# An encoder trunk on one core: ScalarE's weight casts ordered behind sigmoids, VectorE's combinations ordered behind low parts, sums of squares taken ahead, and last stores in finer pieces

## Chip, cores and metric

The kernel runs on one core of one Trainium2 chip. The metric is the device time of one execution in microseconds. Shorter is better. Engines are named as in the profile: PE is TensorE, DVE is VectorE, ACT is ScalarE, POOL is GpSimd, and SP is the engine that issues most DMAs.

## What is computed

One layer of a bidirectional hybrid encoder on x of shape (1, 1024, 1024), everything in float32. Cut to what matters here:

```python
h = rmsnorm(x)
proj = h @ w_in                       # 8192 columns: gated unit, q, v, z_f, z_b, gates
a = glu(glu_in)                       # values * sigmoid(gates), 512 columns
a = dwconv31(a); a = silu(layernorm(a)); a = a @ pw_w
o = bi_hgrn2(q, v, z_f, z_b)          # gated linear recurrence in both directions
b = (headnorm(o) * silu(og)) @ o_w
x = x + (sigmoid(g_a) * a + sigmoid(g_b) * b) @ w_out
x = x + (silu(dwconv3(h2 @ w_gate)) * (h2 @ w_up)) @ w_down     # h2 = rmsnorm(x)
return rmsnorm(x)                     # the last norm, the last stage of the kernel
```

## The kernel before

Activations are kept transposed, with features on the 128 partitions and positions along the row, in two halves of 512 positions. A product of float32 precision is made of three passes of TensorE: every weight and every activation is split into a high part (a cast on ScalarE) and a low part (the source minus the high part, on VectorE). The helper `split` (line 123, its instructions at L124) issues both, and `mm3` (L148, L149, L150) the three matmuls: high by high, high by low, low by high. So a weight's low part is first needed by the third matmul of a job.

The program goes through stages: first norm, gated unit, the other projections ("pairs") with the depthwise convolution on VectorE beside them, layer norm, scan of the heads, output projections, feed-forward network up and down, last norm. TensorE's instructions run exactly in the order in which the program emits them. The other engines' orders are made by a planner at compile time from its own cost model. Once made, each engine's order is fixed, and each engine waits in order. `pin` keeps single instructions in program order, and `tc.issue_after(ins)` makes every instruction of its block that is on the engine of `ins` follow `ins` in that engine's order. It adds no wait on another engine.

**Gated unit (`glu_jobs`, line 916).** There are four groups of 128 columns, 0 to 3. For each group and half there is a gate job and a value job (`glu_tiles`, line 863), each of 24 matmuls into one bank tagged "mm", of which there are three. At the end of a gate job `evac_b` (line 848) applies the sigmoid on ScalarE (L851) from the bank into a page of the tag "tm", of which there are four. At the end of a value job `evac_a` (line 855) multiplies bank and page on VectorE (L857). The first half of all groups and the second half of group 3 run first, while the second norm is still going on; the second halves of groups 0, 1 and 2 come last, as six jobs: gate 0, value 0, gate 1, value 1, gate 2, value 2. In the texts below "gate job 1" means gates of group 1, second half.

`run_jobs` (line 194) prepares a job's weights (`std_job`, line 250: a 512 KB load into one of two "wr" pages, then a split into two of four "wp" pages) just after the job before it has been started in program order. So when the weights of gate job 1 are prepared, the last sigmoid that has been emitted is that of gate job 0. Two "wp" pages belong to a job, so a cast can't run before the job two places ahead has used its pages for the last time.

**Combinations (`h_combos`, line 937).** The pairs use a product scheme with seven products in place of eight. Their operands are sums and differences of quarters of h. For each of four blocks k, three quarters are loaded from DRAM into pages "su" (four of them) and `combos` (line 461) makes three combinations on VectorE (L466), each of which is then split. All four are emitted ahead of the last 17 steps of the gated unit:

```python
p1 = tc.alloc_tile_pool(name="p1", bufs=1, reuse_waits="tile")
h_combos()
s_glu.fill(GLU_LATE)          # GLU_LATE = 17
pair0 = in_pair(0)
w_pair0 = pair0[0]()          # weights of the first pair
s_glu.drain()
```

**Convolution (`conv_steps`, line 1028).** 31 taps of 1024 positions for each of four groups on VectorE (L1036, L1039), emitted between steps of the pairs. A pair's results are evicted by VectorE too (L800), and some by ScalarE. The convolved rows go out to DRAM (`d_cv`) and come back for the layer norm (first sums at L1051 and L1053).

**Last norm (`turn_out`, `finish`, `scale_out`, lines 1904 to 1960).** The last matmuls make blocks of 128 features for groups of 128 positions ("chunks"); the very last part has the second half's chunks 2 and 3, for i = 0 to 7 in turn. Each block is transposed by TensorE (L1912), ScalarE squares it and adds up (L1914), and VectorE applies the gain (L1929). After block 7 a reduction over the eight sums (L1920), a scaling (L1923) and a power on GpSimd (L1924) give the reciprocal root. Then `scale_out` multiplies each chunk, 640 columns on VectorE (L1957) and 384 on ScalarE (L1955), and stores it (L1959, 512 KB). `finish(*PARTS[-1], late=0)` does so for the last two chunks, and with their stores the kernel ends.

Of the kernel before, what the change touches and what calls it, by code (L numbers as in the profile page):

```python
# [10 lines left out]
F32 = mybir.dt.float32  # L11
# [3 lines left out]
AF = mybir.ActivationFunctionType  # L15
ALU = mybir.AluOpType
AX = mybir.AxisListType

P = 128
# [10 lines left out]
GLU_LATE = 17  # L30
ALIGN = 128
H = 512
EPS = 1e-6
# [14 lines left out]
def tile_hybrid_encoder(  # L48
# [22 lines left out]
    nc = tc.nc  # L71
    PSUM = bass.MemoryType.PSUM
    V, A, G, T = nc.vector, nc.scalar, nc.gpsimd, nc.tensor

    S, D = x.shape[1], x.shape[2]
    ND = D // P
    CW = conv_dw_w.shape[2]
# [8 lines left out]
    cp = ctx.enter_context(tc.tile_pool(name="const", bufs=1))  # L86
# [7 lines left out]
    def nm(s):  # L94
        uid[0] += 1
        return f"{s}_{uid[0]}"
# [3 lines left out]
    def bank(tag):  # L100
        return ps.tile([P, H], F32, tag=tag, name=nm(tag), bufs=BANKS[tag])

    def page(pool, tag, bufs, dt=F32):
        return pool.tile([P, H], dt, tag=tag, name=nm(tag), bufs=bufs)

    def tmp():
        return page(mp, "tm", 4)
# [13 lines left out]
    pin = tc.keep_in_program_order  # L121

    def split(hi, lo, src, eng, late=False):
        parts = A.copy(hi, src), eng.tensor_tensor(lo, src, hi.bitcast(F32), op=ALU.subtract)  # L124
        if late:
            for i in parts:
                pin(i)
        return hi, lo

    def w_cols(w, r0, nk, c0, cols=P):  # L130
        return w[0, r0 : r0 + nk * P, c0 : c0 + cols].rearrange("(k p) e -> p k e", p=P)

    def raw_w(src, nk):
        t = mp.tile([P, nk, P], F32, tag="wr", name=nm("wr"), bufs=2)
        nc.sync.dma_start(t, src)
        return t

    def w_page(nk, pool=None):
        if pool is None:
            return mp.tile([P, nk, P], F32R, tag="wp", name=nm("wp"), bufs=4)  # L140
        return pool.tile([P, nk, P], F32R, tag="wq", name=nm("wq"), bufs=3)

    def mm3(acc, w, act, k, first, last, again=False):


        whi, wlo = w
        ahi, alo = act
        T.matmul(acc, whi[:, k, :], ahi, start=first, stop=False, skip_group_check=again)  # L148
        T.matmul(acc, whi[:, k, :], alo, start=False, stop=False, skip_group_check=again)  # L149
        T.matmul(acc, wlo[:, k, :], ahi, start=False, stop=last, skip_group_check=again)  # L150
# [99 lines left out]
    def std_job(src, nk, acts, evac, halves=(0, 1), step=2):  # L250


        def prep():
            raw = raw_w(src, nk)
            return split(w_page(nk), w_page(nk), raw, V)

        def run(w, halves=halves):
            for half in halves:
                acc = bank("mm")
                for k in range(nk):  # L260
                    mm3(acc, w, acts(k, half), k, k == 0, k == nk - 1)
                    if k % step == step - 1 or k == nk - 1:
                        yield
                evac(half, acc)

        return prep, run
# [194 lines left out]
    def combos(ops, k, b11, b12, b22, alloc):  # L461

        def sub(o, a, b):
            V.tensor_tensor(o, a, b, op=ALU.subtract)  # L466

        def parts(i, src):
            ops[i].append(split(alloc(), alloc(), src, V))

        t3 = page(mp, "tm", 4)
        sub(t3, b12, b22)
        parts(7, t3)
        sub(b22, t3, b11)
        parts(6, b22)
        sub(b12, b11, b12)
        parts(5, b12)
# [104 lines left out]
    def in_cols(c0):  # L582
        return w_cols(w_in, 0, ND, c0)
# [3 lines left out]
    ht = {i: [] for i in range(1, 8)}  # L587
# [256 lines left out]

    gate = {}
    early = []

    def evac_b(j):
        def evac(hf, acc):
            gate[j, hf] = tmp()  # L850
            A.activation(gate[j, hf], acc, AF.Sigmoid)  # L851

        return evac

    def evac_a(j):
        def evac(hf, acc):
            V.tensor_tensor(  # L857
                gl[j][:, PAD + hf * H : PAD + (hf + 1) * H], acc, gate.pop((j, hf)), op=ALU.mult
            )

        return evac

    def glu_tiles(j, halves):
        yield std_job(in_cols(CW + j * P), ND, h_std, evac_b(j), halves)
        yield std_job(in_cols(j * P), ND, h_std, evac_a(j), halves)

    glu_raw, glu_w = [], []

# [47 lines left out]
    def glu_jobs():  # L916
        def loaded(job, key, pages):
            def prep():
                return split(pages(), pages(), early[key], V)

            return prep, job[1]

        def early_page():
            return p0.tile([P, ND, P], F32R, tag="xn", name=nm("wp"), bufs=4)

        yield glu_first()
        job0, job1 = glu_tiles(1, (0,))
        yield loaded(job0, 0, early_page)
        yield loaded(job1, 1, lambda: w_page(ND))
        job0, job1 = glu_tiles(2, (0,))  # L930
        yield loaded(job0, 2, lambda: w_page(ND))
        yield job1
        yield from glu_tiles(3, (0, 1))
        for j in (0, 1, 2):
            yield from glu_tiles(j, (1,))

    def h_combos():
        def hy():
            return page(p1, "hy", 24, F32R)

        for k in range(NK2):
            b11, b12, b22 = (page(p1, "su", 4) for _ in range(3))
            for t, (kk, half) in ((b11, (k, 0)), (b12, (k, 1)), (b22, (k + NK2, 1))):
                nc.sync.dma_start(t, d_h[kk][half])
            combos(ht, k, b11, b12, b22, hy)

    s_glu = Stream(run_jobs(glu_jobs(), prime=1, first=GLU_LEAD))
    s_glu.fill()
    ahead = p0.tile([P, ND, P], F32, name="ahead")
# [13 lines left out]
    s_glu.fill(GLU_MORE)  # L963
    p0.release()
    p1 = tc.alloc_tile_pool(name="p1", bufs=1, reuse_waits="tile")
    h_combos()
    s_glu.fill(GLU_LATE)
    pair0 = in_pair(0)
    w_pair0 = pair0[0]()
    s_glu.drain()  # L970
# [85 lines left out]
    for half in range(2):  # L1056
# [18 lines left out]
        rs = next(rstd)  # L1075
# [387 lines left out]
    for h in range(NH):  # L1463
# [4 lines left out]
        for half in range(2):  # L1468
            i = 2 * h + half
# [238 lines left out]
    for k in range(NK2):  # L1708
        s_out.fill(16 if k else 17) if k < NK2 - 1 else s_out.drain()
        b11, b12, b21, b22 = x2[k][0], x2[k][1], x2[k + NK2][0], x2[k + NK2][1]  # L1710
# [193 lines left out]
    def turn_out(i, half, chunks):  # L1904

        t, n = xr[i][half], len(chunks)
        if i == 0 and chunks[0] == 0:
            out_y.append(fy.tile([P, 4, D], F32, tag="y", name=nm("y"), bufs=2))
        ss, y = out_ss[half], out_y[half]
        b = bank(next(y_tags))[:, : n * P]  # L1910
        for m, c in enumerate(chunks):
            T.transpose(b[:, m * P : (m + 1) * P], t[:, c * P : (c + 1) * P], ident)  # L1912
        for m, c in enumerate(chunks):
            A.activation(  # L1914
                out_junk[c % 2], b[:, m * P : (m + 1) * P], AF.Square, accum_out=ss[:, i, c : c + 1]
            )
        those = slice(chunks[0], chunks[-1] + 1)
        if i == ND - 1:
            rs = cp.tile([P, 4], F32, name=nm("frs"), tag="frs", bufs=2)[:, :n]
            V.tensor_reduce(  # L1920
                rs, ss[:, :, those].rearrange("p i c -> p c i"), axis=AX.X, op=ALU.add
            )
            V.tensor_scalar(rs, rs, 1.0 / D, EPS, op0=ALU.mult, op1=ALU.add)  # L1923
            G.tensor_tensor(rs, rs, mhalf.to_broadcast([P, n]), op=ALU.pow)  # L1924
            for m, c in enumerate(chunks):
                out_r[half, c] = rs[:, m : m + 1]

        def gain():
            return V.tensor_tensor(  # L1929
                y[:, those, i * P : (i + 1) * P],  # L1930
                b.rearrange("p (c e) -> p c e", e=P),
                view(fnw, i * P, [[0, n], [1, P]]),
                op=ALU.mult,
            )

        if i == ND - 3 and half and chunks[-1] == 3:
            gains.append(gain)
        elif i == ND - 1:
            pin(gain())
        else:  # L1940
            gain()
# [7 lines left out]

    def scale_out(half, c):  # L1950
        y, r = out_y[half], out_r[half, c]
        for o, cols in ((0, 640), (640, D - 640)):
            sl = slice(o, o + cols)
            if o:
                pin(A.activation(y[:, c, sl], y[:, c, sl], AF.Copy, scale=r))  # L1955
            else:
                pin(V.tensor_scalar(y[:, c, sl], y[:, c, sl], r, None, op0=ALU.mult))  # L1957
        n = half * 4 + c
        nc.sync.dma_start(out[0, n * P : (n + 1) * P, :], y[:, c, :])  # L1959

    out_y, out_r = [], {}
    per_std, per_seven = 2 * ((FIRST + 1) // 2), 7 * ((NS + 1) // 2)
    jobs = std_down(0, FIRST, first_evac)
    first_seven = seven_down(0)[0]
# [53 lines left out]
    n = starts[-1] - per_seven - 12  # L2018
# [50 lines left out]
```

## Time and profile before

| | us |
|---|---|
| median of 3 runs | 1721.52 (1721.14 to 1722.52) |
| the profiled execution's own time | 1721.94 |
| its span in the trace | 1720.0 |
| TensorE busy in the span | 1699.1 |
| VectorE busy | 1256.6 |
| ScalarE busy | 825.0 |
| GpSimd busy | 240.7 |

The span is what the trace covers; the execution's own time has 1.94 us more around it. A row of a timeline gives start and duration in us, engine, line, operation and operands by tile name; in brackets stands how long the engine sat idle before it and what ended that. In the list of waits a row says who waited for whom, for how long in all, how often, and the longest. A row of a table by stretches has the stretch, its length, the busy time of TensorE, weight loads, VectorE, ScalarE and GpSimd with the number of instructions, then TensorE's granted clock, the share of the DMA engines and GB/s. "SPq" is a DMA issue on SP's queue.

### The profile page before, as it was taken

What the parts mean: (1) busy time and instruction counts of PE and PEld (TensorE: products, weight loads), DVE (VectorE), ACT (ScalarE), POOL (GpSimd) and SP (SyncE); (2) the same over time, 40 slices, a digit from 0 to 9 for tenths busy, and PEclk for the clock granted to TensorE, in tenths of its full rate; (3) what the DMA queues carried; (4) which work ended last, traced back from release to release, by engine and by line L of the source; (5) the groups of instructions that cost most, each with busy time, mean ns of one, the idle gap of its engine ahead of it and who ended that gap; (6) DMA issues with size and microseconds to landing.
All of it is one profiled execution on the core that took longest, in us unless ns stands there. A gap on an engine that the chain in (4) does not pass through costs nothing.

```text
span 1720.0 us, 30762 instructions
## 1 busy us (share of the span) xinstructions
PE 1699.1 (99%) x11902; PEld 1416.2 (82%) x11902; DVE 1256.6 (73%) x1937; ACT 825.0 (48%) x1544; POOL 240.7 (14%) x281
## 2 busy tenths in 40 slices
PE   8999999999999999999999999999999999999998
PEld 6878888788788888888888888888888888888787
DVE  4599999745779888888656466667777776657865
ACT  6443443233577777776442245444434433542334
POOL 1212222200001111111100002122222222000110
PEclk9999999999999999999999999999999999999999
DMA  8777888854673444435689466577778776783842
GB/s 281 238 181 177 201 191 189 203 160 148 202 261 91 146 127 133 128 116 200 223 277 279 143 205 199 147 159 153 165 166 174 171 172 154 229 266 102 215 95 99
DMA packets 337096, 308.28 MB, mean 179 GB/s; under 512 B 17582, under 2 KB 249142, under 8 KB 336950
## 3 DMA queue, kind: packets, MB, share of 16 engines
q1 hardware_dynamic: 289590, 267.51, 49.1%
q0 software_dynamic: 47360, 38.81, 15.5%
q8 instruction: 93, 1.52, 0.4%
q14 instruction: 53, 0.43, 0.1%
HBM read 201.40 MB, written 87.03 MB: 168 GB/s over the span
## 4 chain that ended last, share of the span: by engine, by line
PE 61%; DVE 1%; ACT 1%; DMA 0%; issue 0%; POOLq 0%; ACTq 0%; SPq 0%; DVEq 0%
PE mm L148 14%; PE mm L150 14%; PE mm L149 14%; PE sc L148 3%; PE sc L150 3%; PE sc L149 3%; PE ob L1375 2%; PE tr L148 1%; PE tr L150 1%; PE tr L149 1%; PE sc L1197 1%; PE sc L1283 1%; PE mm L1334 1%; PE sc L1334 1%; PE ob L1197 0%
## 5 line engine op out<-in xcount | busy, mean ns | idle before, releaser
L148 PE MATMUL mm<-hx,wp 128*128 128x512 f32 x1068 | 426.9, 400 | 2.3 <-ACT tm L851 1.4
L150 PE MATMUL mm<-hx,wp 128*128 128x512 f32 x1068 | 416.9, 390 | 0.5 <-DVE wp L124 0.5
L149 PE MATMUL mm<-hx,wp 128*128 128x512 f32 x1068 | 416.2, 390 | 0.0
L124 ACT CAST wp<-wr 128x1024 fp32r<-128x1024 f32 (+2 forms) x147 | 147.3, 1003 | 217.8 <-PE mm L149 180.3
L148 PEld LDWEIGHTS mm<-hx,wp 128*128 128x128 f32 x1068 | 200.6, 188 | 45.0 <-DVE ev L800 2.2
L150 PEld LDWEIGHTS mm<-hx,wp 128*128 128x128 f32 x1068 | 200.5, 188 | 44.4 <-DVE wp L124 1.6
L149 PEld LDWEIGHTS mm<-hx,wp 128*128 128x128 f32 x1068 | 200.8, 188 | 39.2 <-issue 0.7
L124 DVE TENSOR_TENSOR wp<-wr,wp 128x1024 fp32r<-128x1024 f32 (+2 forms) x145 | 169.1, 1167 | 39.1 <-ACT wp L124 32.7
L1039 DVE SCALAR_TENSOR_TENSOR acc<-gl,v_b,acc 128x1024 f32<-128x1024 f32 x120 | 148.7, 1272 | 0.4
L440 ACT COPY su<-mm 128x512 f32<-128x512 f32 x82 | 47.7, 582 | 80.1 <-PE mm L150 80.1
L1315 POOL DMA_DIRECT2D S<-D x64 | 36.3, 573 | 284.2 <-ACT S L1313 155.6
L1144 DVE TENSOR_TENSOR qF<-qF,tb 128x512 f32<-128x512 f32 x96 | 65.5, 684 | 13.3 <-ACT A L1178 12.7
L124 ACT CAST wq<-sw 128x1024 fp32r<-128x1024 f32 x41 | 43.2, 1053 | 61.2 <-PE mm L149 32.9
L148 PE MATMUL tr<-hx,wp 128*128 128x512 f32 x180 | 70.5, 392 | 0.0
L150 PE MATMUL tr<-hx,wp 128*128 128x512 f32 x180 | 70.1, 389 | 0.0
L149 PE MATMUL tr<-hx,wp 128*128 128x512 f32 x180 | 70.0, 389 | 0.0
L1144 DVE TENSOR_TENSOR kG<-kG,tb 128x512 f32<-128x512 f32 x96 | 65.5, 685 | 4.7 <-ACT A L1178 2.5
L1652 DVE SCALAR_TENSOR_TENSOR tm<-gp,v_a,tm 128x512 f32<-128x512 f32 x88 | 66.0, 750 | 4.0 <-ACT tm L1650 2.0
L301 POOL DMA_DIRECT2D sw<-in_ffn_w_up_dram x38 | 49.8, 1498 | 116.5 <-DMA sw<-in_ffn_w_up_dram 76.7
L148 PE MATMUL mm<-hy,wp 128*128 128x512 f32 x164 | 64.2, 391 | 0.0
L148 PE MATMUL sc<-hy,wq 128*128 128x512 f32 x164 | 64.2, 391 | 0.0
L150 PE MATMUL sc<-hy,wq 128*128 128x512 f32 x164 | 63.8, 389 | 0.0
(375 smaller groups left out, 3723.3 us busy)
## 6 DMA issues: line engine op xcount, KB each, us to landing
wr<-in_w_in_dram SPq DMA_DIRECT2D x48, 512.0 KB, 5.0
wr<-in_ffn_w_up_dram SPq DMA_DIRECT2D x22, 512.0 KB, 5.1
sw<-in_w_in_dram SPq DMA_DIRECT2D x38, 256.0 KB
d_g<-ft SPq DMA_DIRECT2D x38, 256.0 KB, 2.0
sw<-in_ffn_w_up_dram SPq DMA_DIRECT2D x38, 256.0 KB, 3.5
sw<-in_ffn_w_up_dram POOLq DMA_DIRECT2D x38, 256.0 KB, 6.2
wr<-sw POOLq DMA_DIRECT2D x32, 256.0 KB, 3.3
wr<-wr POOLq DMA_DIRECT2D x32, 256.0 KB, 3.4
```

The costliest lines, as they stand in the source:

```text
L124: parts = A.copy(hi, src), eng.tensor_tensor(lo, src, hi.bitcast(F32), op=ALU.subtract)
L148: T.matmul(acc, whi[:, k, :], ahi, start=first, stop=False, skip_group_check=again)
L149: T.matmul(acc, whi[:, k, :], alo, start=False, stop=False, skip_group_check=again)
L150: T.matmul(acc, wlo[:, k, :], ahi, start=False, stop=last, skip_group_check=again)
L301: G.dma_start(o, a, accum_op=ALU.add)
L440: A.copy(t, acc)
L1039: V.scalar_tensor_tensor(acc, g[:, k : k + S], tap(k), acc, op0=ALU.mult, op1=ALU.add)
L1144: return V.tensor_tensor(o, a, b, op=op)
L1315: G.dma_start(S_t[g : g + 32, :, g : g + 32], D_t[g : g + 32])
L1334: T.matmul(u[:, sl], kTs[d][:, sl], v[:, c, :], start=True, stop=True)
L1375: T.matmul(o[:, sl], l, r, start=(n == 0), stop=(n == len(terms) - 1))
L1652: V.scalar_tensor_tensor(c, g[:, o + k : o + k + H], vec("fdw", k * NF + j), c, op0=ALU.mult, op1=ALU.add,)
```

## The change

Four edits, which add no TensorE work:

1. Each weight preparation of the six last jobs of the gated unit is wrapped in `behind_gate`: the cast must follow, on ScalarE, the sigmoid that was emitted last.
2. For value job 1 and gate job 2 the low part's instruction is kept (`kept_lo`). The combinations of block 2 must follow, on VectorE, the low part of value job 1, and those of block 3 the low part of gate job 2. So that these exist, the gated unit's steps are emitted in between; the later fill is shortened by as many steps.
3. The sums of squares of blocks 0 to 6 are reduced, scaled and given the epsilon when block 6 is done; after block 7 one operation adds the last square to that.
4. In the very last part, chunk 2 is scaled and stored in two pieces, 320 columns on VectorE first, then the rest.

```diff
     gate = {}
     early = []
+    last_gate, last_lo = [], []
...
             gate[j, hf] = tmp()
-            A.activation(gate[j, hf], acc, AF.Sigmoid)
+            last_gate[:] = [A.activation(gate[j, hf], acc, AF.Sigmoid)]
...
+    def behind_gate(job):
+        def prep():
+            with tc.issue_after(last_gate[0].ins):
+                return job[0]()
+
+        return prep, job[1]
+
+    def kept_lo(src, job):
+        def prep():
+            raw, hi, lo = raw_w(src, ND), w_page(ND), w_page(ND)
+            A.copy(hi, raw)
+            last_lo.append(V.tensor_tensor(lo, raw, hi.bitcast(F32), op=ALU.subtract))
+            return hi, lo
+
+        return prep, job[1]
...
         for j in (0, 1, 2):
-            yield from glu_tiles(j, (1,))
+            job0, job1 = glu_tiles(j, (1,))
+            yield behind_gate(kept_lo(in_cols(CW + j * P), job0) if j == 2 else job0)
+            yield behind_gate(kept_lo(in_cols(j * P), job1) if j == 1 else job1)
...
-            combos(ht, k, b11, b12, b22, hy)
+            if k >= 2:
+                while len(last_lo) < k - 1:
+                    s_glu.fill()
+                    fills.append(k)
+                with tc.issue_after(last_lo[k - 2].ins):
+                    combos(ht, k, b11, b12, b22, hy)
+            else:
+                combos(ht, k, b11, b12, b22, hy)
...
+    fills = []
     h_combos()
-    s_glu.fill(GLU_LATE)
+    s_glu.fill(GLU_LATE - len(fills))
...
+        if i == ND - 2:
+            part = cp.tile([P, 4], F32, name=nm("fpt"), tag="fpt", bufs=2)[:, :n]
+            V.tensor_reduce(
+                part, ss[:, : ND - 1, those].rearrange("p i c -> p c i"), axis=AX.X, op=ALU.add
+            )
+            V.tensor_scalar(part, part, 1.0 / D, EPS, op0=ALU.mult, op1=ALU.add)
+            out_part[half, chunks[0]] = part
         if i == ND - 1:
             rs = cp.tile([P, 4], F32, name=nm("frs"), tag="frs", bufs=2)[:, :n]
-            V.tensor_reduce(
-                rs, ss[:, :, those].rearrange("p i c -> p c i"), axis=AX.X, op=ALU.add
+            V.scalar_tensor_tensor(
+                rs,
+                ss[:, i, those],
+                1.0 / D,
+                out_part.pop((half, chunks[0])),
+                op0=ALU.mult,
+                op1=ALU.add,
             )
-            V.tensor_scalar(rs, rs, 1.0 / D, EPS, op0=ALU.mult, op1=ALU.add)
...
-        for o, cols in ((0, 640), (640, D - 640)):
+        n = half * 4 + c
+        rows = out[0, n * P : (n + 1) * P, :]
+        early = 320 if half and c == 2 else 0
+        if early:
+            pin(V.tensor_scalar(y[:, c, :early], y[:, c, :early], r, None, op0=ALU.mult))
+            nc.sync.dma_start(rows[:, :early], y[:, c, :early])
+        for o, cols in ((early, 640 - early), (640, D - 640)):
             sl = slice(o, o + cols)
-            if o:
+            if o == 640:
...
-        n = half * 4 + c
-        nc.sync.dma_start(out[0, n * P : (n + 1) * P, :], y[:, c, :])
+        nc.sync.dma_start(rows[:, early:], y[:, c, early:])
```

More of the change, by code (lines that the diff above doesn't have):

```diff
@@ L1957, in scale_out @@
                 pin(V.tensor_scalar(y[:, c, sl], y[:, c, sl], r, None, op0=ALU.mult))
-        n = half * 4 + c
-        nc.sync.dma_start(out[0, n * P : (n + 1) * P, :], y[:, c, :])
-    out_y, out_r = [], {}
+        nc.sync.dma_start(rows[:, early:], y[:, c, early:])
+    out_y, out_r, out_part = [], {}, {}
     per_std, per_seven = 2 * ((FIRST + 1) // 2), 7 * ((NS + 1) // 2)
```

## Prediction

> **What bounds the kernel now.** I read the totals of the page first, then the list of whom TensorE waited for, then the stretches.
>
> ```profile
> PE 1699.1 (99%) x11902; PEld 1416.2 (82%) x11902; DVE 1256.6 (73%) x1937; ACT 825.0 (48%) x1544; POOL 240.7 (14%) x281
> ```
>
> TensorE is busy 1699.1 of 1720.0 us, and the change touches none of its instructions. So only stalls can go, about 21 us in all. Two stretches (columns: stretch, its length, then busy time of TensorE, weight loads, VectorE, ScalarE, GpSimd) hold most of them, 6.5 at the start and 8.3 at the end:
>
> ```profile
> 0.00:20.00 20.00, 13.51 (x48) 10.32 (x49) 9.13 (x19) 12.79 (x23) 6.50 (x22) 1.00 0.95 305
> ...
> 1680.00:1720.00 40.00, 31.75 (x252) 30.38 (x250) 20.20 (x52) 17.39 (x96) 2.42 (x3) 0.93 0.27 106
> ```
>
> The list of waits, for TensorE alone, names the one stall that the gated unit owns:
>
> ```profile
> PE mm L148 <- ACT tm L851: 1.4, 1, 1.4
> ...
> PE mm L148 <- DVE ev L800: 0.7, 1, 0.7
> ```
>
> The timelines of TensorE and of ScalarE show its place (columns: start, duration, engine, line, what):
>
> ```profile
> 95.77 0.39 PE L149 MATMUL mm<-hx,wp 128*128 128x512 f32 x1
> 96.00 0.39 PE L150 MATMUL mm<-hx,wp 128*128 128x512 f32 x1
> 97.84 0.50 PE L148 MATMUL mm<-hx,wp 128*128 128x512 f32 x1 [1.45 <-ACT tm L851]
> ```
>
> ```profile
> 68.38 1.05 ACT L124 CAST wp<-wr 128x1024 fp32r<-128x1024 f32 x1 [3.30 <-PE mm L149]
> 74.20 0.60 ACT L851 ACTIVATE tm<-mm 128x512 f32<-128x512 f32 x1 [4.76 <-PE ob L519]
> ...
> 85.43 1.05 ACT L124 CAST wp<-wr 128x1024 fp32r<-128x1024 f32 x1
> ...
> 90.80 1.05 ACT L124 CAST wp<-wr 128x1024 fp32r<-128x1024 f32 x1 [3.28 <-PE mm L149]
> ...
> 96.24 1.04 ACT L124 CAST wp<-wr 128x1024 fp32r<-128x1024 f32 x1
> 97.19 1.08 ACT L851 ACTIVATE tm<-mm 128x512 f32<-128x512 f32 x2
> ```
>
> Two sigmoids run together at 97.19. The first belongs to gate job 0 (second half). Its sums were complete when the cast at 85.43 started, because that cast waits for the same job to free its weight page. The sigmoid stands behind three more weight casts in ScalarE's order and holds one of three "mm" banks until 97.7, so value job 1 can't start. Matmuls follow each other here at 0.23 us, so from 96.00 to 97.84 the loss is 1.84 - 0.23 = **1.61 us**.
>
> Next, VectorE:
>
> ```profile
> 120.00:240.00 120.00, 120.00 (x531) 99.35 (x530) 119.72 (x130) 50.67 (x72) 27.82 (x26) 1.00 0.84 190
> ```
>
> The third busy number is VectorE: 119.72 of 120. In the convolution stage it is as full as TensorE, and three rows show the two tied together at its end:
>
> ```profile
> 327.52 2.60 DVE L1039 SCALAR_TENSOR_TENSOR acc<-gl,v_b,acc 128x1024 f32<-128x1024 f32 x2
> ...
> 339.54 0.69 DVE L1053 TENSOR_TENSOR tm<-tm,cx 128x512 f32<-128x512 f32 x1 [6.50 <-DMA cx<-d_cv]
> ...
> 341.15 0.68 DVE L800 TENSOR_TENSOR ev<-su,mm 128x512 f32<-128x512 f32 x1
> ```
>
> ```profile
> 341.41 0.39 PE L150 MATMUL sc<-hx,wq 128*128 128x512 f32 x1
> 341.88 0.50 PE L148 MATMUL mm<-hx,wp 128*128 128x512 f32 x1
> ```
>
> The last convolution tap ends at 330.1. Its result goes out and comes back, and the sums at 339.54 wait for it. The eviction at 341.15 stands behind them, and the matmul at 341.88 starts 0.47 after the one before instead of 0.23: it waited for that eviction. So TensorE at 342 can come earlier only by as much as VectorE's convolution ends earlier.
>
> **The change, part by part.** *Casts behind sigmoids.* No instruction is added; ScalarE's order changes. The sigmoid of gate job 0 goes ahead of the cast at 85.43, where nothing holds it, which frees the bank 11 us earlier. The cast moves back one sigmoid, 0.60, against 5 us until its job needs it: no cost. The 1.61 us go. One cast meets a real wait: that of gate job 0 itself, at 68.38, must now follow the sigmoid at 74.20. It ends near 75.9, its low part on VectorE near 77, and job 0 starts near 80: hidden, with 3 us to spare.
>
> *Combinations behind low parts.* This too only orders VectorE:
>
> ```profile
> 69.47 1.22 DVE L124 TENSOR_TENSOR wp<-wr,wp 128x1024 fp32r<-128x1024 f32 x1 [5.53 <-ACT wp L124]
> ...
> 80.11 0.69 DVE L857 TENSOR_TENSOR gl<-mm,tm 128x512 f32<-128x512 f32 x1 [1.18 <-PE mm L150]
> ...
> 89.47 0.81 DVE L1036 TENSOR_SCALAR acc<-gl,v_b,v_a 128x1024 f32<-128x1024 f32 x1
> 91.78 0.69 DVE L466 TENSOR_TENSOR tm<-su,su 128x512 f32<-128x512 f32 x1 [1.50 <-DMA su<-d_h]
> ...
> 95.99 1.22 DVE L124 TENSOR_TENSOR wp<-wr,wp 128x1024 fp32r<-128x1024 f32 x1
> ...
> 102.62 1.22 DVE L124 TENSOR_TENSOR wp<-wr,wp 128x1024 fp32r<-128x1024 f32 x1
> ```
>
> The low part of value job 1 (95.99, ends 97.2) is needed by that job's third matmul. With the stall gone that is 96.23 + 2 x 0.23 = 96.7, so 0.5 us of stall would come back; the low part of gate job 2 (102.62) likewise. The change puts both ahead of the third and fourth combinations: the first right behind its cast (90.80 + 1.05 = 91.85), the second behind its own, near 97.9.
>
> Now what VectorE gains, since that is the limit at 342. Its work is the same. Gate job 0's low part (1.22) moves from idle time at 69.47 into the 1.18 of idle before 80.11, which cancels. Left is the 1.50 of idle at 91.78, where the third combination waited for its loads. Job 1's low part and job 0's gating product, both later before, now run there, and those loads have landed meanwhile. Best case: taps fill every hole and 1.50 is gained. Worst: no tap is placed between, VectorE waits from 90.3 to about 91.1 for value job 0 (it frees the page for the cast at 90.80 with its last matmuls), 0.2 for the cast, then 1.0 for the second low part (the combination's six operations of 0.6 to 0.7, as at 91.78, from 93.1 end near 96.9, against 97.9) and up to 0.7 for the fourth combination's loads: 2.7 in place of 1.50, 1.2 lost. I take **1.2 gained**, nearer the full 1.50, because the planner put a tap at 89.47 into just such a hole. TensorE gains the smaller of 1.61 and that.
>
> *The end.*
>
> ```profile
> 1712.12 0.42 DVE L1929 TENSOR_TENSOR y<-tr,fnw 128x256 f32<-128x256 f32 x1 [0.18 <-ACT oj L1914]
> 1712.92 0.18 DVE L1920 TENSOR_REDUCE frs<-os 128x2 f32<-128x16 f32 x1 [0.38 <-ACT oj L1914]
> 1713.13 0.17 DVE L1923 TENSOR_SCALAR frs<-frs 128x2 f32<-128x2 f32 x1
> 1713.21 0.42 DVE L1929 TENSOR_TENSOR y<-sc,fnw 128x256 f32<-128x256 f32 x1
> 1714.20 1.01 DVE L1957 TENSOR_SCALAR y<-y,frs 128x640 f32<-128x640 f32 x2 [0.57 <-POOL frs L1924]
> ```
>
> ```profile
> 1714.20 1.12 ACT L1955 ACTIVATE y<-y,frs 128x384 f32<-128x384 f32 x2 [1.32 <-POOL frs L1924]
> 1714.84 0.84 SPq L1959 DMA_DIRECT2D out_dram<-y  x2
> ```
>
> After the last squares (1712.9) two dependent small operations, 1712.92 to 1713.30, become one. Its form isn't in the trace at two columns; the nearest rows are 0.17 and 0.18, so it ends near 1713.10: **0.20 gained**. The two operations added for the first seven tiles (0.35) fit the 0.38 of idle before 1712.92. If they slip behind it, the 0.20 is gone.
>
> The stores: each is 512 KB.
>
> ```profile
> 1715.50:1715.75 0.25, 0.00 (x0) 0.00 (x0) 0.00 (x0) 0.00 (x0) 0.00 (x0) 0.50 0.45 180
> ...
> 1716.00:1716.25 0.25, 0.00 (x0) 0.00 (x0) 0.00 (x0) 0.00 (x0) 0.00 (x0) 0.50 0.99 393
> ...
> 1718.25:1718.50 0.25, 0.00 (x0) 0.00 (x0) 0.00 (x0) 0.00 (x0) 0.00 (x0) 0.50 0.11 33
> ```
>
> Data flows without a hole from about 1715.64 to 1718.3 at some 393 GB/s, so the end is set by when the flow starts, 0.80 behind the first issue (1714.84). That issue waits for ScalarE's 384 columns, 0.6 after the root. The new first piece, 320 columns of VectorE, needs (0.55 - 0.17) x 320/636 + 0.17 = 0.36, so it starts about 0.28 earlier and carries 160 KB, 0.42 of flow. The second can follow by then (0.75 after the root: SP's issue takes 0.33), the third as before. 0.28 goes, less a guess of 0.05 for 128 more packets: **0.23**, between nothing and 0.3. VectorE's three operations end level with ScalarE's two. The Trainium skill (DMA: Bandwidth & Descriptors, Rules for kernel authors) speaks against it: join small transfers, each carries a fixed part, about 2.0 us there. If pieces paid that in turn the end would be some 2 us later; the row at 1716.00, full while one store follows the other, shows that they overlap.
>
> Sum: 1.2 + 0.20 + 0.23 = **1.63 us**. The span of 1720.0 becomes 1718.4 and the profiled execution's 1721.94 becomes 1720.3. The median of the runs is 0.42 below that execution, so the forecast is 1721.52 - 1.6 = **1719.9**.
>
> **The rivals.** *Swallowed.* VectorE gains nothing at 91.78, so TensorE waits at 342 for what it won at 97. For it: 119.72 of 120 and the tie at 341.88. Against: the idle of 1.50 is real. Only the end is left, 0.43: 1721.1. The Trainium skill (Perfetto Trace Analysis, Identifying the Most-Contended Engine) would have it so: improve the engine with the highest occupancy, which in this stage is hardly TensorE alone.
>
> *More.* VectorE gains all, the evictions meet TensorE in better order, and the later losses go too: 0.7 at L800 and 0.24 at 342 beside 1.61 and 0.43, 3.0 in all with up to 0.4 for others tied to them: 1718.3.
>
> *Slower: SP's queue.* The rows:
>
> ```profile
> 70.72 0.38 SPq L135 DMA_DIRECT2D wr<-in_w_in_dram  x1
> 71.15 0.58 SPq L374 DMA_DIRECT2D sw<-in_w_in_dram  x1
> ...
> 72.44 2.98 SPq L378 DMA_DIRECT2D sw<-in_w_in_dram  x1
> ```
>
> ```profile
> sw<-in_ffn_w_up_dram SPq DMA_DIRECT2D x38, 256.0 KB, 3.5
> ```
>
> The load at 70.72 is issued when gate job 0's low part ends (70.7). That is now 77. If it keeps its place in the queue, the loads of the first pair behind it move 6.3 us, and VectorE's sum of them, near 80.7 in its order, waits: 5.3 us lie between the last issue (75.4) and it, of which I count 3.5 for landing, as for the later loads of that size, so 6.3 - 1.8 = 4.5. Less the 1.5 and the 0.43, 2.6 later: 1724.1. It decides from 1.8 us of delay on. Against: the planner can issue those loads first, as they wait for nothing.
>
> *Not done:* if the sigmoid still waits for a page of the same four "tm" buffers, nothing moves but the end: 1721.1.
>
> **How the numbers follow.** Forecast 45%, swallowed 20%, more 14%, slower 13%, not done 4%, other order elsewhere 4%. A change of 0.2%, 3.4 us, is about what a measurement of this kernel can tell from none. The range runs from 1717.9 (just past "more") to 1722.6 (the worst case of VectorE's holes, 1.2 - 0.4 = 0.8 later, with some spread); most of "slower" lies outside. Faster by over 0.2% (below 1718.1) takes half of "more" and some of the rest, 0.09; slower (above 1725.0) the upper part of "slower" and some of the rest, 0.11; within, 0.80.
>
> **What would show it.** Right: a sigmoid near 85.5, no wait of L148 for L851, the low part right behind 91.9, VectorE's hole at 91.8 gone, the last tap near 328.9 and three stores, the first about 0.5 earlier. Wrong: a last tap still at 330.1 or later with TensorE waiting near 342 (swallowed), pair loads issued after 77 (slower), or a part sum of squares that ends after 1712.9.

## The result and the profile after

The changed kernel took 1726.2 us (median of 9 runs, 1724.5 to 1726.8), the kernel before 1721.5 (9 runs, 1720.7 to 1723.7). The ratio is 1.0022, with a 95% interval of 1.0014 to 1.0031: some 3.8 us slower by the ratio (the medians lie 4.7 apart), where 1.6 faster was forecast. Medians and ratios here and below leave out one slow run, of the experiment e2, which took 2426.9 us at a granted clock of 0.66. The profiled execution of the changed kernel took 1724.5 us, with a span of 1722.5.

TensorE's busy time is the same (1699.2 against 1699.1), so the loss is again stalls. The table by stretches shows where. First the kernel before (its middle stretch stands in the prediction), then the changed one; the first busy number is TensorE, the third VectorE:

```profile
80.00:120.00 40.00, 38.55 (x170) 31.38 (x169) 38.38 (x53) 19.54 (x27) 5.44 (x9) 1.00 0.68 190
...
240.00:350.00 110.00, 109.11 (x479) 89.37 (x479) 95.89 (x93) 37.22 (x51) 22.69 (x21) 1.00 0.81 196
```

```profile
80.00:120.00 40.00, 39.63 (x174) 32.21 (x173) 38.25 (x61) 19.51 (x29) 6.13 (x9) 1.00 0.76 206
120.00:240.00 120.00, 118.11 (x516) 96.28 (x516) 118.69 (x122) 49.63 (x71) 27.32 (x25) 1.00 0.81 183
240.00:350.00 110.00, 108.44 (x478) 89.42 (x477) 97.03 (x94) 37.75 (x51) 22.70 (x21) 1.00 0.82 195
```

The gated unit's stretch gained 1.1 us of TensorE, as meant. The next stage, which the diff doesn't touch, lost 1.9 and 0.7. TensorE's waits in the changed kernel name the cause, and its timeline the places:

```profile
PE mm L148 <- DVE ev L800: 3.3, 3, 1.6
```

```profile
129.61 0.50 PE L148 MATMUL mm<-hx,wp 128*128 128x512 f32 x1 [0.53 <-DVE ev L800]
...
169.67 0.50 PE L148 MATMUL mm<-hx,wp 128*128 128x512 f32 x1 [1.25 <-DVE ev L800]
...
324.27 0.50 PE L148 MATMUL mm<-hx,wp 128*128 128x512 f32 x1 [1.56 <-DVE ev L800]
```

Before there was one such wait, of 0.7 (at 303); the wait for the sigmoid (1.4 at L851) is gone. VectorE's timeline shows why the evictions are late. First the changed kernel, then the kernel before, at the same two pairs:

```profile
127.74 1.22 DVE L124 TENSOR_TENSOR wq<-sw,wq 128x1024 fp32r<-128x1024 f32 x1
128.87 0.68 DVE L800 TENSOR_TENSOR ev<-su,mm 128x512 f32<-128x512 f32 x1
...
166.59 1.23 DVE L124 TENSOR_TENSOR wq<-sw,wq 128x1024 fp32r<-128x1024 f32 x1 [0.35 <-ACT wq L124]
167.74 1.28 DVE L1066 SCALAR_TENSOR_TENSOR acc<-gl,v_b,acc 128x1024 f32<-128x1024 f32 x1
168.93 0.68 DVE L800 TENSOR_TENSOR ev<-su,mm 128x512 f32<-128x512 f32 x1
```

```profile
129.84 0.67 DVE L800 TENSOR_TENSOR ev<-su,mm 128x512 f32<-128x512 f32 x1
130.43 1.21 DVE L124 TENSOR_TENSOR wq<-sw,wq 128x1024 fp32r<-128x1024 f32 x1
...
167.75 0.67 DVE L800 TENSOR_TENSOR ev<-su,mm 128x512 f32<-128x512 f32 x1
168.35 1.21 DVE L124 TENSOR_TENSOR wq<-sw,wq 128x1024 fp32r<-128x1024 f32 x1
```

Each pair ends its second accumulator with an eviction of (su, mm), and TensorE's next product needs that "mm" bank. The next pair's column weights need a low part ("wq<-sw,wq"). Before, the planner put the eviction first. With the gated unit's order changed it put the low part first in the first four pairs, so the eviction came 1.1 us later (127.74 to 128.87), or 2.3 where a tap slipped between too (166.59 to 168.93). At the third wait, 324.27, the low part stands first in both kernels, but VectorE has fallen back and the eviction comes at 323.54, against 321.73 before.

### The profile page after: what moved, and what is told of

Read it like the earlier page. It is cut to its first block, busy times and chain, and to the rows that moved or that the text cites. A ratio compares the mean times of both kernels' runs of the same rounds, so it can differ in the third digit from the quotient of the medians.

```text
span 1722.5 us, 30760 instructions
## 1 busy us (share of the span) xinstructions
PE 1699.2 (99%) x11902; PEld 1414.6 (82%) x11902; DVE 1257.6 (73%) x1941; ACT 825.0 (48%) x1544; POOL 240.9 (14%) x281
## 4 chain that ended last, share of the span: by engine, by line
PE 60%; DVE 1%; DMA 1%; ACT 1%; issue 1%; POOLq 0%; SPq 0%; DVEq 0%; ACTq 0%
PE mm L148 14%; PE mm L150 14%; PE mm L149 14%; PE sc L148 3%; PE sc L150 3%; PE sc L149 3%; PE ob L1402 2%; PE tr L148 1%; PE tr L150 1%; PE tr L149 1%; PE sc L1224 1%; PE sc L1310 1%; PE mm L1361 1%; PE sc L1361 1%; DMA wr<-in_ffn_w_down_dram 1%
## 5 line engine op out<-in xcount | busy, mean ns | idle before, releaser
L148 PE MATMUL mm<-hy,wp 128*128 128x512 f32 x164 | 64.3, 392 | 0.0
L148 PE MATMUL sc<-hy,wq 128*128 128x512 f32 x164 | 64.2, 392 | 0.0
L149 PE MATMUL mm<-hy,wp 128*128 128x512 f32 x164 | 63.8, 389 | 0.0
```

## The experiments

Three theories were set against each other. **A**: the loss is the order of VectorE in the stage after the gated unit, evictions behind low parts. **B**: it is VectorE's work, since gate job 0's low part moved from idle time into the full stretch. **C**: it is the finer stores at the end. Later **S** and **T** were two readings of the end. A useful second measure beside the median is when TensorE starts its last transposes in each profiled execution. It can't tell much less than 1 us, since at 73 us, ahead of everything that was changed, the traces already lie between 72.2 and 73.9.

| kernel | median us | ratio to before, 95% | last transposes at |
|---|---|---|---|
| before | 1721.8, 1722.3, 1722.1 (three chips) | 1 | 1711.75 |
| changed | 1726.2 | 1.0022 [1.0014, 1.0031] | 1714.16 |
| e1: edit 1 alone | 1743.7 | 1.0122 [1.0108, 1.0136] | 1734.61 |
| e2: edit 2 alone | 1723.2 | 1.0006 [0.9996, 1.0015] | 1712.41 |
| e3: edits 3 and 4 | 1723.0 | 1.0004 [0.9995, 1.0013] | 1711.61 |
| e4: edits 1 and 2 | 1726.0 | 1.0020 [1.0011, 1.0029] | 1714.15 |
| e5: e4, group 0 left as before | 1723.6 | 1.0012 [1.0003, 1.0021] | 1712.24 |
| e6: before, evictions held back | 1732.1 | 1.0059 [1.0046, 1.0071] | 1724.62 |
| e7: changed, evictions first | 1720.9 | 0.9994 [0.9985, 1.0002] | 1711.02 |
| e8: before, evictions first | 1721.9 | 1.0000 [0.9991, 1.0008] | 1711.45 |
| e9: e5 and edit 3, evictions first | 1720.2 | 0.9985 [0.9977, 0.9994] | 1710.22 |
| e10: edit 2, evictions first | 1719.6 | 0.9984 [0.9975, 0.9993] | 1710.26 |
| e11: e7 without edit 4 | 1720.5 | 0.9991 [0.9982, 1.0000] | 1710.77 |
| e12: edit 4 alone | 1722.5 | 1.0002 [0.9993, 1.0011] | 1710.69 |

**The parts alone (e1 to e4).** e1 has the six `behind_gate` wraps only, e2 the `kept_lo` jobs and the waits of the combinations for them, e3 the sums of squares and the last stores, e4 both orders without the end.

> Edit 1 alone: the weight casts of the six last gated-unit jobs behind the last sigmoid, nothing else. Theory A (order of evictions: VectorE's planned order now has a pair's eviction (1,1) behind the low part of the next pair's column weights, and TensorE waits for its bank): this kernel's order has two such places in the first four pairs against four with the whole change and none before, so about half of the loss, +1 to +3 us against before. Theory B (VectorE's work: gate job 0's low part, 1.2 us, has moved out of idle time into the full stretch): the whole loss of the orders, +3 to +5. Theory C (the finer stores at the end): no loss, -1.5 to 0.

> Edit 2 alone: combinations 2 and 3 behind the two low parts, with the gated unit's steps emitted in between; casts are free. Theory A: three evictions of the first four pairs stand behind a low part (one of them behind a convolution tap too), so +2 to +4 us against before. Theory B: gate job 0's low part stays in idle time, so no loss, -1.5 to +0.5. Theory C: -1.5 to 0.

> Edits 3 and 4 alone: the early sum of squares and the finer last stores. VectorE's order in the convolution is that of before. Theories A and B: between -0.5 and +0.2 us, as the power starts 0.25 earlier and the flow 0.45 earlier but the end didn't follow in the one trace. Theory C (three stores take longer to be confirmed than two): +1 to +4 us.

> Edits 1 and 2 together, the end as before. Theories A and B: nearly the whole loss, +3.5 to +5 us. Theory C: -1.5 to 0.

C is out as the cause of the loss: both orders without the end (e4) lose as much as the whole change, and e3's loss, 0.7 us by the ratio, isn't clear of noise. e2 met neither forecast: by the ratio it is 1.0 us slower, between B's range and A's, and its interval just includes no change. Edit 1 alone costs 21 us, which no theory had. Its list of TensorE's waits and ScalarE's timeline:

```profile
PE mm L148 <- ACT wp L124: 8.6, 1, 8.6
PE mm L150 <- DVE wp L124: 6.1, 2, 5.6
```

```profile
97.49 0.59 ACT L852 ACTIVATE tm<-mm 128x512 f32<-128x512 f32 x1
97.98 1.03 ACT L124 CAST wp<-wr 128x1024 fp32r<-128x1024 f32 x1
```

Gate job 0's sigmoid runs at 97.49, where the sigmoids ran before. So putting the casts behind it doesn't bring it forward: in ScalarE's order something other than these casts keeps it back. What that is no run shows; a page of the four "tm" buffers, which sigmoids and combinations share, is one candidate. That is the outcome of the prediction's rival "not done", but with a price it did not see: the cast of gate job 1 now stands behind that sigmoid, and TensorE waits 8.6 and 5.6 us for weights.

e2, without edit 1, does bring it forward. Its sigmoid of gate job 0 runs at 85.27, its TensorE list has no wait for L852, and its stretch of the gated unit is full in TensorE and VectorE:

```profile
84.31 1.05 ACT L124 CAST wp<-wr 128x1024 fp32r<-128x1024 f32 x1
85.27 0.58 ACT L852 ACTIVATE tm<-mm 128x512 f32<-128x512 f32 x1
```

```profile
80.00:120.00 40.00, 40.00 (x178) 33.15 (x177) 39.96 (x61) 19.82 (x29) 6.18 (x9) 1.00 0.83 206
```

So edit 1 needs edit 2, but edit 2 doesn't need edit 1.

**Whose work it is (e5).** Edits 1 and 2, but the first two jobs keep their casts:

```diff
-            yield behind_gate(kept_lo(in_cols(CW + j * P), job0) if j == 2 else job0)
-            yield behind_gate(kept_lo(in_cols(j * P), job1) if j == 1 else job1)
+            yield behind_gate(kept_lo(in_cols(CW + j * P), job0) if j == 2 else job0) if j else job0
+            yield behind_gate(kept_lo(in_cols(j * P), job1) if j == 1 else job1) if j else job1
```

> Both orders, but the casts of gate job 0 and value job 0 are left as in the kernel before, so gate job 0's low part stays in VectorE's idle time at 69.5 and only the later jobs' casts stand behind a sigmoid. Theory B (the low part that moved from 69.5 to 74.9 adds 1.2 us to VectorE's full stretch, and with it the loss): the loss of 4.2 us shrinks to that of the combinations alone, 1722 to 1723.5. Theory A (VectorE's order in the next stage, where evictions of the second accumulator stand behind the next pair's column low part): the low parts are still ahead of the evictions in four of the first pairs here, so the time stays at 1724 to 1726.5, and TensorE waits for the evictions some 2 to 3.5 us in all.

1723.6 lies between the two forecasts and decides nothing as a time. Its stretches do:

```profile
80.00:120.00 40.00, 40.00 (x178) 33.13 (x177) 39.96 (x61) 19.83 (x29) 6.18 (x9) 1.00 0.83 204
120.00:240.00 120.00, 118.64 (x521) 97.23 (x520) 118.53 (x122) 49.26 (x70) 27.31 (x25) 1.00 0.81 185
```

In the gated unit TensorE and VectorE are full: 40.00 and 39.96, where the changed kernel has 39.63 and 38.25. So B is right on that stage: group 0's casts behind sigmoids cost VectorE 1.7 us of idle time there. But the next stage still loses 1.4 us of TensorE, with 2.6 us of waits for evictions, as A has it, although only three of the first four pairs have the low part first here and not four.

**The order itself (e6 to e8).** e6 is the kernel before, with the evictions of the first four pairs (HELD is 0 to 3) put behind the next pair's low part; nothing of the diff is in it.

```diff
+            if n in HELD and e == 1 and len(quadrant) == 4:
+                with tc.issue_after(q_lo[n + 1].ins):      # low part of the next pair's columns
+                    evs[e](*quadrant)
```

> The kernel before with one thing of the changed kernel's order and none of its edits: in the first four pairs of the convolution stage the eviction of (su, mm) is issued behind the next pair's column low part. Theory A: TensorE waits for that eviction in several pairs, about 1 us each, and the time rises by 2 to 4 us, to 1723.5 to 1725.5. Theory B, or any other cause in the stage before: no change, 1721 to 1722.5.

e7 is the changed kernel with the opposite: for twelve pairs that low part is emitted later, once the eviction is there, and issued behind it. e8 does so to the kernel before.

```diff
+            elif behind is not None:
+                w[1], w[2] = both(rows, None)
+                sums()
+                a22 = quadrant()
+                yield 7
+                with tc.issue_after(ev11[behind].ins):     # eviction of (su, mm), pair before
+                    w[7], w[5] = both(col, pool)
+                w[6], w[3] = both(rows, None)
```

> The changed kernel with all its edits, and in the first twelve pairs the next pair's column low part issued behind the eviction of (su, mm), as the kernel before has it in most pairs. Theory A: TensorE's waits for the evictions fall from 3.3 us to under 1.2, and the loss goes: 1720.5 to 1723, the forecast's side of the loss if the gain of the stage before is kept. Theory B: the late start stays, 1724.5 to 1726.5.

> The control of the run before it: the kernel before with the same rule for the first twelve pairs, which changes its own order in the last pairs of the stage only. Both theories: 1721 to 1722.5, no more than 0.1% from the kernel before; a larger difference would be the price of the later emission of those pages, to be taken off the run before it.

e7 and e8 came out as A says. In e7 the first pair's eviction stands ahead of the low part again, TensorE's list has no wait for L814 (the former L800) at all, and the middle stretch is full:

```profile
128.08 0.68 DVE L814 TENSOR_TENSOR ev<-su,mm 128x512 f32<-128x512 f32 x1
128.68 1.21 DVE L127 TENSOR_TENSOR wq<-sw,wq 128x1024 fp32r<-128x1024 f32 x1
```

```profile
80.00:120.00 40.00, 39.19 (x172) 31.68 (x171) 37.82 (x59) 18.75 (x28) 6.13 (x9) 1.00 0.76 202
120.00:240.00 120.00, 120.00 (x531) 99.29 (x530) 119.33 (x125) 51.67 (x72) 27.30 (x26) 1.00 0.82 184
240.00:350.00 110.00, 109.86 (x485) 90.68 (x484) 97.80 (x96) 38.03 (x51) 22.55 (x22) 1.00 0.84 203
```

The whole loss is regained. By the medians e7 is 1.5 us faster than the kernel before on its chip (1.0 by the ratio), but its interval just includes no change. The control e8 gains nothing, so it isn't the later emission. Nor is it that e7 also turns round the pairs near 302 and 321, where the kernel before has the low part first: e8 turns them round too. B predicted that e7 stays at 1724.5 or more. It falls as the cause of the loss, though it holds for the gated unit.

e6 went the way of A, but by 10 us and not by 2 to 4. Two of its waits are long. The rows of TensorE and VectorE, and the stretches behind the first wait:

```profile
132.16 0.50 PE L152 MATMUL mm<-hx,wp 128*128 128x512 f32 x1 [2.08 <-DVE ev L805]
...
133.36 0.63 PE L153 MATMUL mm<-hx,wp 128*128 128x512 f32 x1
133.79 0.63 PE L154 MATMUL mm<-hx,wp 128*128 128x512 f32 x1
...
312.84 0.79 PE L152 MATMUL mm<-hx,wp 128*128 128x512 f32 x1 [4.50 <-DVE ev L805]
```

```profile
310.31 0.69 DVE L1064 TENSOR_TENSOR tm<-cx 128x512 f32<-128x512 f32 x1 [5.20 <-DMA cx<-d_cv]
310.91 1.28 DVE L1052 SCALAR_TENSOR_TENSOR acc<-gl,v_b,acc 128x1024 f32<-128x1024 f32 x1
312.11 0.68 DVE L805 TENSOR_TENSOR ev<-su,mm 128x512 f32<-128x512 f32 x1
```

```profile
132.00:133.00 1.00, 0.84 (x4) 0.71 (x5) 1.00 (x3) 0.81 (x2) 0.00 (x0) 0.98 0.11 29
133.00:134.00 1.00, 1.00 (x4) 0.81 (x3) 1.00 (x2) 0.43 (x1) 0.00 (x0) 0.50 1.01 291
```

The wait of 4.50 isn't A's mechanism: here the planner put a layer-norm sum, which waits 5.20 us for a transfer, ahead of the eviction. So e6 shows that holding evictions back costs time, and how easily the same planner adds another order, but it is no clean price for the low parts alone. The clock is taken up below.

**The best of it, and the end (e9 to e12).** If A is right and B holds for the gated unit, the best version leaves group 0's casts alone and puts evictions first.

> Both orders without gate job 0's and value job 0's casts behind sigmoids, the column low parts of the first twelve pairs behind the evictions of (su, mm), the squares summed ahead, and the stores as in the kernel before: the candidate for the fastest. Theory A (only the order of the evictions cost time; the gain of the stage before is there to be kept): 1719.5 to 1721.5, no PE wait for the evictions over 0.8 us. Rival (leaving gate job 0 in the idle time changes what the evictions' order gives): 1722 to 1724. At the end, theory S (SyncE's issues in a row set the end): from the last transposes to the end 8.0 us, against 8.25 before and 8.38 with the finer stores.

> The combinations behind low parts alone, with the column low parts behind the evictions of (su, mm) in the first twelve pairs. Alone the combinations gave 1723.3. Theory A: TensorE's 2.4 us of waits for the evictions go and 1.5 to 3 us come off, 1720 to 1722; from the last transposes to the end 8.25 us as before. Rival (the loss of the combinations alone lies in their own stage): 1722.5 to 1724.

Both are faster than the kernel before: 1720.2 and 1719.6, ratios 0.9985 and 0.9984, some 2.7 us, with intervals below 1. So edit 2 with evictions first is enough; e10 has nothing of edits 1, 3 and 4. Its median lies 0.4 below A's range. e10's stretches are full in both engines, and its TensorE list has one wait for L814 left, of 1.0 at the end of the stage:

```profile
80.00:120.00 40.00, 40.00 (x178) 33.12 (x177) 39.96 (x61) 19.85 (x29) 6.18 (x9) 1.00 0.81 205
120.00:240.00 120.00, 120.00 (x531) 99.36 (x530) 119.15 (x123) 50.33 (x71) 27.89 (x26) 1.00 0.80 185
```

Against e7 and e11, which have group 0's casts behind sigmoids, they start the last transposes 0.7 us earlier (mean of two and two); the medians' intervals overlap, so this is likely and not shown. At the end e9 meets the 8.0 us that S expected (8.05).

e11 takes the finer stores out of e7, e12 puts them alone into the kernel before (the diff of `scale_out` above, undone and done).

> The changed kernel with the evictions of (su, mm) first, as two runs ago, but the last stores whole as in the kernel before; the squares are still summed ahead. Theory S (SyncE issues stores one after the other, 0.42 us each, so a third issue gives back what the earlier power gained): from the last transposes to the end 8.0 us, 0.25 less than before. Rival T (the last bytes' confirmation is late whenever the stores start earlier): 8.3 to 8.4 us. The median, 1720 to 1722, can't tell the two apart; the profile can, since the seven profiles without the edits at the end agree within 0.04 us.

> The kernel before with the finer stores alone; the squares are summed as before. Theory S: the first store is issued 0.2 us earlier and the last 0.2 us later; from the last transposes to the end 8.5 to 8.7 us, against 8.25. Rival T: 8.3 to 8.4 us. The forecast's own step, that the end comes with the first store: 8.0 us. The median within 0.1% of the kernel before in all cases.

From the start of the last transposes to the span's end the seven profiles without edits 3 and 4 that were there by then (before, e1, e2, e4, e5, e6, e8) have 8.27 to 8.30 us, and e10 8.29 (spans in ns, as the traces have them). With both edits it is 8.38 (changed and e7) and 8.42 (e3); with the earlier sums alone 8.06 (e11) and 8.05 (e9); with the finer stores alone 8.66 (e12). S's numbers (8.0, and 8.5 to 8.7) were met, and T's and those of the forecast's own step were not. But the traces don't bear out S as the mechanism. SyncE's issues in the changed kernel:

```profile
1716.78 0.33 SPq L1995 DMA_DIRECT2D out_dram<-y  x1
1717.21 0.87 SPq L2002 DMA_DIRECT2D out_dram<-y  x2
```

Counted from the last transposes, the first issue is at 2.62 (before: 3.09), and the third ends at 3.92, where the second ended before (3.93). All the same the bytes are through earlier: the stores' data flows from 3.44 to 6.33, before from 3.92 to 6.79. Before, the data ended at 1718.5. In the changed kernel it ends at 1720.49, though the span is 2.5 us longer:

```profile
1720.25:1720.50 0.25, 0.00 (x0) 0.00 (x0) 0.00 (x0) 0.00 (x0) 0.00 (x0) 0.50 0.21 66
1720.50:1720.75 0.25, 0.00 (x0) 0.00 (x0) 0.00 (x0) 0.00 (x0) 0.00 (x0) 0.50 0.00 0
```

What sets the end comes after the bytes. After its last issue SyncE goes through ten waits in a fixed order, for semaphores on which, among others, the stores report. A row of this view has line, engine, operation and count, the shortest, median and longest duration in ns, and the first and the last start. First the kernel before, then the changed one:

```profile
L2064 SPq EVENT_SEMAPHORE  x8: 17/28/28, 1715.7 to 1716.5; - x8
...
L2064 SPq EVENT_SEMAPHORE  x2: 28/28/28, 1717.6 to 1719.1; - x2
```

```profile
L2107 SPq EVENT_SEMAPHORE  x8: 28/28/28, 1720.9 to 1721.6; - x8
```

Before, the last store reports on the semaphore that SyncE waits for last, and the eight waits ahead of the stores' two run while data flows. In the changed kernel the third store, by the semaphore's number in the trace, reports on one that SyncE waits for third. That wait is over at 6.70 from the last transposes, before at 7.39; but seven more follow it one after the other, and the last starts at 7.48. From the last wait to the end it is 0.89 to 0.91 us in all fourteen traces. The ten with two stores have no wait behind the last store's, the four with three stores have seven, which take 0.46 to 0.79. In e12 too the last store's wait is over earlier than before (7.31), and the end is later by the waits behind it. So S had the right numbers by luck: it is the place of the last store's semaphore among the closing waits, and not the third issue, that gives back the gain. No run moved that semaphore, so what the finer stores would gain without this is open.

## Why the prediction was wrong

**"Where nothing holds it": this step failed.** TensorE no longer waits for the sigmoid, which runs at 84.70, and the low part of value job 1 runs at 91.32, as the prediction has it:

```profile
84.70 0.59 ACT L852 ACTIVATE tm<-mm 128x512 f32<-128x512 f32 x1
```

```profile
91.32 1.22 DVE L879 TENSOR_TENSOR wp<-wr,wp 128x1024 fp32r<-128x1024 f32 x1
93.96 0.69 DVE L466 TENSOR_TENSOR tm<-su,su 128x512 f32<-128x512 f32 x1 [1.42 <-DMA su<-d_h]
```

But it isn't edit 1 that did this, as the prediction's order of ScalarE had it. With edit 1 alone the sigmoid stays at 97.49 (e1); with edit 2 alone it runs at 85.27 (e2). No run shows a gain from edit 1, and it is what moved gate job 0's low part out of idle time.

**"I take 1.2 gained": this step failed, twice.** First, in the gated unit VectorE gained nothing. The hole of 1.50 was to close because the loads would have landed; the row at 93.96 still has 1.42 of idle. Those loads were issued 2.8 us later, for the "su" pages come free from the earlier combinations, and these had been pushed back by gate job 0's low part, now at 74.88 (where that cast stays, in e5, there is no hole). First the kernel before, then the changed one:

```profile
85.50 2.08 SPq L944 DMA_DIRECT2D su<-d_h  x2
```

```profile
88.31 1.66 SPq L963 DMA_DIRECT2D su<-d_h  x2
```

The step "moves into the 1.18 of idle, which cancels" was thus wrong: the idle was used, but what stood behind it in the queue moved too. For edit 2 alone the forecast of VectorE was near: in e2 VectorE gains 1.6 us of busy time between 80 and 120 (39.96 against 38.38).

Second, and this is the loss: the step let TensorE gain "the smaller of 1.61 and that", as if the next stage's order stayed. A planner that orders whole engines from its own costs gave another order there, and the evictions fell behind the low parts: waits of 0.7 became 3.3, and on VectorE the last tap ended at 332.0, against 330.1. e7 shows the size: with that order taken back the same edits give 1.0 to 1.5 us less than before. That this is near the 1.6 of the forecast is in part luck, since the sum is made otherwise: the sigmoid's stall and the L800 wait go, while VectorE gains nothing in the gated unit and the finer stores lose. The only rival that covered it, "other order elsewhere", had 4% and no price.

The Trainium skill (PSUM — Partial Sum Buffer, Engine vs sequencer instructions) says that VectorE's queue is strictly first in, first out. The traces agree: the eviction at 128.87 starts only as the low part of 127.74 to 128.96 goes through. The prediction had used this for its own stage and not for the next.

**The end.** "0.20 gained" by one operation fewer was right: the power starts 0.25 earlier after the last transposes (1.47 against 1.72), and e11's end comes 0.23 earlier (8.06 against 8.29). "0.23 gained" by the finer first store was right for the flow of data and wrong for the end. With both edits the flow starts 0.48 earlier and ends 0.46 earlier, where 0.43 was forecast; the guess of 0.05 for more packets fits, as the flow takes 2.87 to 3.01 us with three stores and 2.86 to 2.88 with two. The step that failed is "so the end is set by when the flow starts": behind the bytes stand the closing waits, and seven of them now come after the last store's. Alone, the finer stores cost 0.37 (e12). The Trainium skill (DMA: Bandwidth & Descriptors, Rules for kernel authors), which the prediction weighed and put aside, would join small transfers. The end came out its way, by 0.32 to 0.37 us for the extra piece (8.38 against 8.06, 8.66 against 8.29), but the traces show no fixed part that each piece pays. The 2.0 us that the prediction takes from that page stand in another section (Anatomy of one DMA — SWDGE (gpsimd) path), for DMAs that GpSimd issues, and SyncE issues these.

**The rivals.** "SP's queue" did not occur: the first pair's loads were issued at 69.3 to 70.9, ahead of the load that waits for gate job 0 (76.1). "Swallowed" was right that VectorE gains nothing, but put the end of that at 342 and at no loss. "Not done" is right of edit 1 alone, where the sigmoid stays, but at a cost of 21 us.

## What to carry to other kernels

Where a planner orders an engine, an edit that only moves instructions is a new order for the stages behind it too; compare the order of the evictions there before counting any gain, and fix it by hand where an accumulator's next use hangs on it. A wait that is put on an in-order engine costs what stands behind it, also when its own slot was idle. Run each edit alone before they are joined: here one of two did the work, and the other took part of it back. At the very end of a kernel, the last byte isn't the end: look which waits stand behind that of the last store.

## What the runs showed of the hardware

A stall of TensorE can cost more than its length. After the wait of 2.08 us in e6 the granted clock fell to 0.50 at about 133, and from 132.96 to 136.35 the matmuls started 0.43 us apart in place of 0.23: eight of them, about 8 x 0.20 = 1.6 us on top. After the wait of 4.50 it was the same until 317, and in e1 after a wait of 1.97, at 302.10, the clock was 0.50 from about 303 to 306.5. The changed kernel's waits of 1.25 and 1.56 left it at 1.00 in the 4 us before and behind. The Trainium skill (TensorE: Matmul & The Clock Gate, Part 1) has the clock at half after an idle window of about 3.4 us; here the stretch at half speed lasted about that long, but 2.08 and 1.97 us of idle were enough.
